# The second half of the last gate, computed as Strassen block products

## The chip, the cores and the metric

One core of a Trainium2 chip runs one launch of one layer of a decoder trunk. The metric is the device time of that launch in microseconds; several runs are summed up by their median. Engines are named as in the profile: PE multiplies matrices, DVE and ACT do elementwise work, POOL does a little arithmetic and issues some DMAs, SP issues most DMAs.

## The reference

Only the end of the layer matters here. `x` is the residual stream after the feed-forward block, 576 tokens (512 of the prompt, 64 of the samples) of 1024 channels.

```
x = x + _rmsnorm(f, g_ffn_post)                                    # f: the feed-forward block
x = x + jax.nn.sigmoid(_rmsnorm(x, g_ple) @ w_ple_gate) * (p_l @ w_ple_proj)
return x                                                           # y_prompt and y_sample
```

`w_ple_gate` is 1024x1024. It is "the last gate" of the title. All arithmetic is float32.

## The kernel before

**Layout.** Activations lie channel-major: a tile is 128 channels x 576 tokens, and each product runs over the two token halves of `H = 288` columns (half 0 and half 1). A product in float32 is made of three matmuls in the type fp32r, which split each operand into a high and a low part: high x high, high x low, low x high. A plain tile of 128 output channels by 576 tokens over 1024 input channels takes 8 x 3 x 2 = 48 matmuls of 288 columns. Weights come by SP's DMAs as raw float32 (`wst`), ACT makes the high part (`whi`, a cast), DVE the low part (`wlo`, a subtraction). Four `whi` and four `wlo` buffers of 1024 columns exist, so weights are made a few tiles ahead.

**Block products.** Most other matrix products of the kernel already use a Strassen scheme. `panels()` lists the weight tiles in their order; `two(a, b, kind)` marks two neighbouring output tiles as a pair. A pair cuts its problem into 2x2 blocks (two output tiles, two halves of the input channels, two token halves) and makes it with 7 block products of 12 matmuls instead of 8. It needs four weight blocks and four sums of weight blocks (class `Pair`), and, for each of four channel tiles, four sums of activations (class `Operands`). For a pair of kind "sum" the weight sums are made ahead in device memory by POOL's accumulating DMAs (`weight_sums`), eight for each pair of 256 KB, two at each `tick`; a tick is a tiny POOL copy that follows the cast of a weight tile. `Operands.make` takes channel tiles j and j + 4, makes four chained sums of 288 columns on DVE (`stmp`), and splits them into high (ACT) and low (DVE) parts (`xs`): the first sum alone, then the other three as one 864-column piece. `pairs()` runs the products; the results of the four blocks are called c11, c12 (in place in their PSUM banks), c21 and c22 (one more DVE subtraction, `value`).

**The last stage.** `handover(..., nxt)` ends the feed-forward block and starts the gate. It finishes four tiles of `f`, adds them into the residual (`residual`, lines 1149 and 1150), scales and splits the result by `g_ple` (`split_gain`, lines 578 and 579) into `XH`, `XL`, then runs the gate's tiles 0 to 3, first all four on half 0 (`pa`), then all four on half 1 (`pb`). Meanwhile `squares` sums the squares of the residual in `ssn` (DVE line 1132), and `stats(ssn, rn, i)` turns them into the factor 1/rms of half i: one matmul with a constant matrix into a PSUM bank (line 566), a DVE transpose out of that bank (548), a DVE step (554), a power on POOL (555), three DVE steps (556, 557, 560) and a transpose into `rn` (562). Only with `rn` can `evac_y` (lines 1260 to 1264) take a finished tile out of its PSUM bank: multiply by `rn` (DVE), tanh (ACT), two DVE steps with `pp` and the residual, a DMA to the output. The normalization is applied after the product, so the matmuls need no `rn`. There are 8 PSUM banks: 6 in the pool `psum`, 2 in `psb`. Tile 4 follows in `handover`, tiles 5 to 7 in the loop at the end; tile 7 is run half by half.

**What sets the order.** A scheduler places the instructions of each engine from dependencies, its own estimates and priorities (`tc.high_priority`). On the chip each engine then takes its list strictly in that order.

Of the kernel before, what the change touches and what calls it, by code (L numbers as in the profile page):

```python
# [9 lines left out]
AF = mybir.ActivationFunctionType  # L10
# [4 lines left out]
SKEW = 4  # L15
WARM = 10
T = 576
H = 288
# [11 lines left out]
def panels():  # L30

    out, items = [], []

    def cols(name, ms, k0=0):
        for m in ms:
            items.append((len(out), "one"))
            out.append([(name, k0 + k, m) for k in range(8)])

    def two(a, b, kind="pair", k0=0):
        items.append((len(out), kind))
        for name, m in (b, a):
            out.append([(name, k0 + k, m) for k in range(8)])

    def small(tiles):
        items.append((len(out), "one"))
        out.append(tiles)

    cols("rq", range(2))  # L50
    cols("rk", range(2))
    cols("rv", range(4))
    for t in (0, 2):
        two(("rg", t), ("rg", t + 1))
    for t in (0, 2):
        for n in ("cc", "ch", "cb"):
            two((n, t), (n, t + 1))
    for n in ("conv", "ret", "att"):
        if n == "ret":
            two(("ak", 0), ("av", 0))  # L60
            for t in (0, 2):
                two(("aq", t), ("aq", t + 1))
        for m in range(0, 8, 2):
            two(("g" + n, m), ("g" + n, m + 1))
            small([("b" + n, k, q) for q in (m, m + 1) for k in range(4)])
    cols("wo", range(8))
    small([("pp", k, m) for m in range(4) for k in range(2)])
    for c in range(4):
        if c == 0:
            cols("f1", range(8))  # L70
            cols("f2", range(8))
            continue
        for m in range(8 * c, 8 * c + 4):
            two(("f1", m), ("f1", m + 4), "sum")
        n = 4 if c < 3 else 2
        for m in range(n):
            two(("f2", m), ("f2", m + n), "pair" if m else "sum", 8 * c)
        cols("f2", range(2 * n, 8), 8 * c)
    small([("pp", k, m) for m in range(4, 8) for k in range(2)])
    cols("pg", range(8))  # L80
    return out, items


# [1 line left out]
def decoder_step(ctx: ExitStack, tc: tile.TileContext, xT, pT, W, consts, smalls, s0q, s0t, ckT, cv,  # L85
# [50 lines left out]
    def halft():  # L136
        return hlf.tile([P, H], F32, tag="hlf", name=nm("hlf"))
# [153 lines left out]
    def need(j, part=None):  # L291

        while not (j in wprep if part is None else j in made and part in made[j].w):
            next(make)
# [208 lines left out]
    def unit(w, xh, xl, kws, ks, half=None):  # L503
        ps = [mbank() if half in (None, i) else None for i in range(2)]
        n = len(ks)
        for q in range(n):
            mm(w, kws[q], ps, xh(ks[q]), xl(ks[q]), q == 0, q == n - 1)
            if q % 4 == 3:
                pump()
        return ps  # L510
# [100 lines left out]
    def later(fs):  # L611
        for f, a in fs:
            yield
            f(*a)
# [516 lines left out]
            A.activation(t, src, AF.Square)  # L1131
            V.tensor_tensor(out=ssx[:, HS[i]], in0=ssx[:, HS[i]], in1=t, op=ALU.add)

    def handover(hin, lin, evac, src, gn, tag, nxt):


        php = pp_inputs()
        pp = bigt(F32, "pp")
        pps.append(pp)
        XH, XL = Act8(F32R, "xh" + tag), Act8(F32R, "xl" + tag)  # L1140
        ra = cpool.tile([P, T], F32, tag="rb", name="ra" + tag)
        rn = npool.tile([P, T], F32, tag="rn", name="rn" + tag)
        ssn = npool.tile([P, T], F32, tag="ssn", name="ssn" + tag)

        def residual(i, ks):
            with tc.high_priority():
                for k in ks:
                    h, t = HS[i], halft()
                    V.tensor_tensor(out=t, in0=src(k)[:, h], in1=ra[:, h], op=ALU.mult)  # L1149
                    V.tensor_tensor(out=X1(k)[:, h], in0=X1(k)[:, h], in1=t, op=ALU.add)  # L1150
                    split_gain(X1(k)[:, h], gn, k, XH(k)[:, h], XL(k)[:, h])

        def squares(i):
            for k in range(8):
                addsq(ssn, X1(k)[:, HS[i]], i, k == 0)

        w = []
        for q in range(SKEW):
            w.append(nextw())
            evac(8 - SKEW + q, unit(w[q], hin, lin, ident_k, ident_k, 0), 0)  # L1160
        bg.append(later([(stats, (evac.ss, ra, 0))]))
        pump()
        for q in range(SKEW):
            ps = unit(w[q], hin, lin, ident_k, ident_k, 1)
            with tc.high_priority():
                evac(8 - SKEW + q, ps, 1)
            residual(0, ((), (0, 1), (2, 3), (4, 5))[q])
        wp = nextw()
        pp_unit(wp, 0, pp, *php)
        residual(0, (6, 7))  # L1170
        pp_unit(wp, 1, pp, *php)
        pp_unit(wp, 2, pp, *php)
        with tc.high_priority():
            stats(evac.ss, ra, 1)
        pp_unit(wp, 3, pp, *php)
        w, pa, pb = [], [], []
        for q in range(SKEW):
            w.append(nextw(2 if q < 2 else 0))
            residual(1, (2 * q, 2 * q + 1))
            pa.append(unit(w[q], XH, XL, ident_k, ident_k, 0))  # L1180
            if q == 2:
                squares(0)
        squares(1)
        for q in range(SKEW):
            pb.append(unit(w[q], XH, XL, ident_k, ident_k, 1))
            if q == 1:
                stats(ssn, rn, 0)
                for i in range(SKEW):
                    nxt(i, pa[i], rn, 0)
        need(items[pos[0]][0])  # L1190
        need(items[pos[0] + 1][0])
        bg.append(later([(stats, (ssn, rn, 1))]))
        pump()
        p4 = unit(nextw(), XH, XL, ident_k, ident_k)
        for q in range(SKEW):
            nxt(q, pb[q], rn, 1)
        for i in range(2):
            nxt(SKEW, p4, rn, i)
        return XH, XL, rn
# [55 lines left out]
                V.scalar_tensor_tensor(t[:, HS[i]], ps[i][:, :H], 0.0, r[:, HS[i]], op0=ALU.max, op1=ALU.mult)  # L1255
                squares_f(m, i, t[:, HS[i]])

    def evac_y(m, ps, r, i):
        z = halft()
        V.tensor_tensor(out=z, in0=ps[i][:, :H], in1=r[:, HS[i]], op=ALU.mult)  # L1260
        A.activation(z, z, AF.Tanh, scale=0.5)
        V.scalar_tensor_tensor(z, z, 1.0, pps[m // 4][:, m % 4, HS[i]], op0=ALU.add, op1=ALU.mult)
        V.tensor_tensor(out=X1(m)[:, HS[i]], in0=X1(m)[:, HS[i]], in1=z, op=ALU.add)
        nc.sync.dma_start(out=yT[:, m, HS[i]], in_=X1(m)[:, HS[i]])

    def block_tile(q, which):

# [94 lines left out]
        nc.sync.dma_start(out=X1.t[k], in_=dx[:, 4 * k:4 * k + 4, :])  # L1362
    nc.sync.dma_start(out=pps[0], in_=dpp)
    fhl = F[0].hi, F[0].lo
    XH, XL, rb = handover(*fhl, evac_f, f, 4, "3", evac_y)


    for m in range(SKEW + 1, 8):
        if m == 7:
            w = nextw()  # L1370
            ps = [unit(w, XH, XL, ident_k, ident_k, i)[i] for i in range(2)]
        else:
            ps = unit(nextw(), XH, XL, ident_k, ident_k)
        for i in range(2):
            evac_y(m, ps, rb, i)

# [111 lines left out]
```

## Time and the profile before

| | us |
|---|---|
| median of 3 runs | 986.15 (986.05 to 987.69) |
| profiled execution, its own time | 987.22 |
| span of the profiled execution, first to last instruction | 985.4 |
| PE busy | 957.6 (97%) |
| DVE busy | 712.6 (72%) |
| ACT busy | 531.5 (54%) |

The profiled execution is 1.07 us above the median. Its span leaves out 1.8 us of its own time. PE is busy nearly throughout; where DVE holds the chain, it is at stage borders.

### The profile page before, as it was taken

What the parts mean: (1) busy time and instruction counts of PE and PEld (TensorE: products, weight loads), DVE (VectorE), ACT (ScalarE), POOL (GpSimd) and SP (SyncE); (2) the same over time, 40 slices, a digit from 0 to 9 for tenths busy, and PEclk for the clock granted to TensorE, in tenths of its full rate; (3) what the DMA queues carried; (4) which work ended last, traced back from release to release, by engine and by line L of the source; (5) the groups of instructions that cost most, each with busy time, mean ns of one, the idle gap of its engine ahead of it and who ended that gap; (6) DMA issues with size and microseconds to landing.
All of it is one profiled execution on the core that took longest, in us unless ns stands there. A gap on an engine that the chain in (4) does not pass through costs nothing.

```text
span 985.4 us, 18290 instructions
## 1 busy us (share of the span) xinstructions
PE 957.6 (97%) x7081; PEld 925.0 (94%) x7081; DVE 712.6 (72%) x1308; ACT 531.5 (54%) x1051; POOL 187.1 (19%) x257
## 2 busy tenths in 40 slices
PE   9999999989989999999999999999999999999998
PEld 9999898989979888799999999999999999999897
DVE  7898789765576776577427878558847965785986
ACT  7345444433345564545436455468558845885642
POOL 0414443433324222332001100000010011000010
PEclk9999999999999999999999999999999999999999
DMA  8637565658779665688522532444486368593112
GB/s 301 168 86 199 165 138 146 163 164 220 194 218 248 143 153 153 143 226 252 187 66 71 223 108 100 155 148 145 120 199 192 110 153 222 164 356 109 65 62 79
DMA packets 65576, 160.45 MB, mean 163 GB/s; under 512 B 8089, under 2 KB 11193, under 8 KB 64241
## 3 DMA queue, kind: packets, MB, share of 16 engines
q1 hardware_dynamic: 48672, 114.75, 34.9%
q0 software_dynamic: 16672, 44.48, 21.8%
q8 instruction: 55, 0.90, 0.4%
q14 instruction: 33, 0.26, 0.1%
q10 hardware_dynamic: 144, 0.06, 0.0%
HBM read 139.17 MB, written 51.55 MB: 194 GB/s over the span
## 4 chain that ended last, share of the span: by engine, by line
PE 77%; DVE 13%; DMA 4%; ACT 2%; issue 2%; POOL 1%; SPq 0%; ACTq 0%; DVEq 0%; POOLq 0%
PE pm L501 31%; PE pbb L329 18%; PE pa L329 12%; PE pe L329 12%; DMA wst<-in_W 3%; DVE wlo L257 3%; POOL rs_b L555 1%; DVE hlf L1149 1%; DVE xl L579 1%; DVE x L1150 1%; DVE wst L227 1%; DVE s L952 1%; PE pb L964 1%; ACT whi L256 1%; DVE wlo L164 1%
## 5 line engine op out<-in xcount | busy, mean ns | idle before, releaser
L257 DVE TENSOR_TENSOR wlo<-wst,whi 128x1024 fp32r<-128x1024 f32 (+1 forms) x180 | 195.4, 1087 | 95.9 <-ACT whi L256 95.1
L256 ACT CAST whi<-wst 128x1024 fp32r<-128x1024 f32 (+1 forms) x180 | 168.3, 940 | 129.9 <-PE pe L329 29.9
L329 PE MATMUL pbb<-xs,whi 128*128 128x288 f32 x1080 | 227.1, 302 | 10.0 <-DVE akv L426 4.1
L329 PEld LDWEIGHTS pbb<-xs,whi 128*128 128x128 f32 x1080 | 174.9, 190 | 19.0 <-DVE akv L426 4.9
L329 PE MATMUL pbb<-xs,wlo 128*128 128x288 f32 x540 | 160.6, 297 | 0.0
L329 PE MATMUL pa<-fq,whi 128*128 128x288 f32 x720 | 147.7, 297 | 0.6 <-DVE fq L583 0.5
L329 PEld LDWEIGHTS pa<-fq,whi 128*128 128x128 f32 x720 | 116.0, 189 | 2.3 <-DVE fq L583 0.7
L329 PE MATMUL pa<-fq,wlo 128*128 128x288 f32 x360 | 106.8, 297 | 0.4 <-DVE wlo L257 0.4
L329 PEld LDWEIGHTS pbb<-xs,wlo 128*128 128x128 f32 x540 | 102.7, 190 | 0.0
L163 ACT CAST whi<-wst 128x1024 fp32r<-128x1024 f32 (+1 forms) x64 | 61.5, 965 | 70.9 <-PE pm L501 48.8
L501 PE MATMUL pm<-xl,whi 128*128 128x288 f32 x384 | 95.0, 299 | 1.5 <-DVE xl L579 1.4
L501 PE MATMUL pm<-xh,whi 128*128 128x288 f32 x384 | 94.9, 300 | 1.5 <-ACT xh L578 1.4
L501 PE MATMUL pm<-xh,wlo 128*128 128x288 f32 x384 | 93.5, 296 | 0.3 <-DVE wlo L164 0.3
L164 DVE TENSOR_TENSOR wlo<-wst,whi 128x1024 fp32r<-128x1024 f32 (+1 forms) x64 | 71.2, 1118 | 23.7 <-ACT whi L163 21.3
L268 POOL COPY pace<-whi 128x1 f32<-128x1 f32 x61 | 36.6, 600 | 240.8 <-ACT whi L256 190.3
L227 DVE TENSOR_TENSOR wst<-wst 128x512 f32<-128x512 f32 x90 | 61.1, 686 | 28.7 <-DMA wst<-in_W 28.0
L555 POOL TENSOR_TENSOR rs_b<-rs_a,mhalf 128x9 f32<-128x9 f32 (+2 forms) x15 | 34.8, 2322 | 222.7 <-DVE rs_a L554 222.7
L329 PE MATMUL pe<-xs,whi 128*128 128x288 f32 x360 | 73.5, 294 | 0.1
L329 PE MATMUL pe<-fq,whi 128*128 128x288 f32 x360 | 73.3, 296 | 0.0
L501 PE MATMUL pm<-fq,whi 128*128 128x288 f32 x384 | 70.4, 296 | 0.0
L329 PEld LDWEIGHTS pa<-fq,wlo 128*128 128x128 f32 x360 | 67.9, 189 | 1.9 <-DVE wlo L257 1.1
L501 PEld LDWEIGHTS pm<-xh,whi 128*128 128x128 f32 x384 | 65.7, 188 | 3.9 <-ACT xh L578 2.4
(280 smaller groups left out, 2025.6 us busy)
## 6 DMA issues: line engine op xcount, KB each, us to landing
wst<-in_W SPq DMA_DIRECT2D x86, 512.0 KB, 4.5
wst<-in_W SPq DMA_DIRECT2D x105, 256.0 KB, 3.3
ts<-in_W POOLq DMA_DIRECT2D x90, 256.0 KB, 5.7
wst<-ts SPq DMA_DIRECT2D x60, 256.0 KB, 3.3
ts<-ts POOLq DMA_DIRECT2D x30, 256.0 KB, 3.5
df<-tmp POOLq DMA_DIRECT2D x16, 288.0 KB, 5.1
x<-in_xT SPq DMA_DIRECT2D x10, 288.0 KB, 4.2
dacc<-tmp SPq DMA_DIRECT2D x8, 288.0 KB, 4.3
```

The lines of the kernel that those rows point to most:

```text
L163: A.copy(out=hi[:, c, :], in_=st[:, c, :])
L164: V.tensor_tensor(out=lo[:, c, :], in0=st[:, c, :], in1=hi[:, c, :].bitcast(F32), op=ALU.subtract)
L227: V.tensor_tensor(out=out, in0=a, in1=b, op=ALU.add)
L256: A.copy(out=hi, in_=r[:, :n, :])
L257: V.tensor_tensor(out=lo, in0=r[:, :n, :], in1=hi.bitcast(F32), op=ALU.subtract)
L268: t = G.tensor_copy(out=pace, in_=hi[:, 0, :1].bitcast(F32))
L329: PE.matmul(bank[:, :H], lhsT=lhs[:, s + j, :], rhs=rhs, start=start and j == 0 and i == 0, stop=j == 3 and i == 2, skip_group_check=True)
L501: PE.matmul(p[:, :H], lhsT=lhs[:, kw, :], rhs=r, start=s, stop=e)
L555: G.tensor_tensor(out=b, in0=a, in1=mhalf[:, :nb], op=ALU.pow)
L579: V.scalar_tensor_tensor(lo, src, gain(gi, k), hi.bitcast(F32), op0=ALU.mult, op1=ALU.subtract)
L952: V.scalar_tensor_tensor(s[:, h, :], dist, -SLOPES[h], p[g][:, i * w:i * w + w], op0=ALU.mult, op1=ALU.add)
L964: PE.matmul(po[grow(g), :], lhsT=avt[:, 128 * chunk + 64 * g:128 * chunk + 64 * g + 64], rhs=sb[g], start=kh == 0, stop=kh == nk - 1)
```

## The change

Tiles 0 to 3 of the gate stay plain. Tiles 4 to 7 become two pairs, (4, 6) and (5, 7), of kind "sum". Their weight sums join the list that POOL's DMAs make, at its end. In `handover`, while the four `pb` tiles are issued, ACT makes the scaled residual of channel tiles q and q + 4 (a copy of 576 columns scaled by the gain) and `Operands.make` makes the sums from it: four sets, q = 0 to 3. The residual's existing `XH`, `XL` serve as the plain blocks. After `stats` of half 1 the two pairs run by `pairs`, and the results go through `evac_y`. `evac_y` now works in a `tmp` buffer (five of 576 columns) instead of `hlf` (three of 288), writes the result there and sends it from there, so that the residual `X1` isn't overwritten while the sums still read it.

```diff
@@ panels()
     small([("pp", k, m) for m in range(4, 8) for k in range(2)])
-    cols("pg", range(8))
+    cols("pg", range(4))
+    for m in (4, 5):
+        two(("pg", m), ("pg", m + 2), "sum")
@@ handover
-    def handover(hin, lin, evac, src, gn, tag, nxt):
+    def handover(hin, lin, evac, src, gn, tag, nxt, sums=None):
...
         for q in range(SKEW):
             pb.append(unit(w[q], XH, XL, ident_k, ident_k, 1))
+            if sums:
+                t = [tmpt() for _ in range(2)]
+                for i in range(2):
+                    A.activation(t[i], X1(q + 4 * i), AF.Copy, scale=gain(gn, q + 4 * i))
+                sums.make(*[[z[:, h] for h in HS] for z in t])
             if q == 1:
                 stats(ssn, rn, 0)
                 for i in range(SKEW):
                     nxt(i, pa[i], rn, 0)
+        bg.append(later([(stats, (ssn, rn, 1))]))
+        pump()
+        if sums:
+            need(items[pos[0]][0], "b21")
+            pump()
+            sums.at = lambda i, k: (XH(k)[:, HS[i]], XL(k)[:, HS[i]])
+
+            def done(q, which):
+                if q.n == 0 and which == "c11":
+                    for i in range(SKEW):
+                        nxt(i, pb[i], rn, 1)
+                m, i = where(which)
+                z = None if which in ("c11", "c12") else halft()
+                evac_y(4 + q.n + 2 * m, None, rn, i, value(q, which, z))
+
+            pairs(2, sums, done, True)
+            rest()
+            return
         need(items[pos[0]][0])
         need(items[pos[0] + 1][0])
-        bg.append(later([(stats, (ssn, rn, 1))]))
-        pump()
         p4 = unit(nextw(), XH, XL, ident_k, ident_k)
@@ evac_y
-    def evac_y(m, ps, r, i):
-        z = halft()
-        V.tensor_tensor(out=z, in0=ps[i][:, :H], in1=r[:, HS[i]], op=ALU.mult)
+    def evac_y(m, ps, r, i, src=None):
+        z = tmpt()[:, :H]
+        V.tensor_tensor(out=z, in0=ps[i][:, :H] if src is None else src, in1=r[:, HS[i]], op=ALU.mult)
         A.activation(z, z, AF.Tanh, scale=0.5)
         V.scalar_tensor_tensor(z, z, 1.0, pps[m // 4][:, m % 4, HS[i]], op0=ALU.add, op1=ALU.mult)
-        V.tensor_tensor(out=X1(m)[:, HS[i]], in0=X1(m)[:, HS[i]], in1=z, op=ALU.add)
-        nc.sync.dma_start(out=yT[:, m, HS[i]], in_=X1(m)[:, HS[i]])
+        V.tensor_tensor(out=z, in0=X1(m)[:, HS[i]], in1=z, op=ALU.add)
+        nc.sync.dma_start(out=yT[:, m, HS[i]], in_=z)
@@ end of the kernel
-    XH, XL, rb = handover(*fhl, evac_f, f, 4, "3", evac_y)
-
-
-    for m in range(SKEW + 1, 8):
...
+    handover(*fhl, evac_f, f, 4, "3", evac_y, Operands(None))
```

How the order of instructions moves, at three places (lines of the changed kernel are shifted by 2 up to `handover` and by 23 in `evac_y`). First PE at the statistics of half 1, before: `pm_11326` and `pm_11327` are the two halves of tile 4, `pb_11352` the bank of the statistics.

```order
L501 MATMUL pm_11326<-xh_10568,wlo_11310 128x288
L501 MATMUL pm_11327<-xh_10568,wlo_11310 128x288
L566 MATMUL pb_11352<-ssn_10574,ones_d 128x288
L501 MATMUL pm_11326<-xh_10569,whi_11309 128x288
L501 MATMUL pm_11327<-xh_10569,whi_11309 128x288
```

PE at the same place, after: `pm_11318` is the last of the four `pb` tiles, `pa_11423` the first block product of the first pair.

```order
L503 MATMUL pm_11318<-xh_10601,whi_11008 128x288
L503 MATMUL pm_11318<-xl_10603,whi_11008 128x288
L503 MATMUL pm_11318<-xh_10601,wlo_11009 128x288
L568 MATMUL pb_11410<-ssn_10606,ones_d 128x288
L331 MATMUL pa_11423<-xh_10600,whi_11399 128x288
```

Half of tile 4 stood ahead of the statistics and is gone from there; the statistics follow the plain tiles directly. PE has 168 matmuls behind them in both kernels; ahead of them, back to the statistics of half 0, 70 before and 50 after, and 4 fewer ahead of those.

Second, DVE from the transpose of half 0's statistics to the factor `rn` of half 0, before (`wlo` is the low part of a weight tile).

```order
L548 STREAM_TRANSPOSE tmp_11223<-pb_11221 128x288
L1132 TENSOR_TENSOR ssn_10574<-ssn_10574,hlf_11168 128x288
L554 TENSOR_SCALAR rs_a_11225<-tmp_11223 128x9
L164 TENSOR_TENSOR wlo_11316<-wst_11314,whi_11315 128x1024
L556 SCALAR_TENSOR_TENSOR rs_d_11227<-rs_b_11226 128x9
L557 TENSOR_TENSOR rs_d_11227<-rs_d_11227,rs_a_11225 128x9
L560 SCALAR_TENSOR_TENSOR tmp_11223<-rs_d_11227,rs_b_11226 128x288
L562 STREAM_TRANSPOSE rn_10573<-tmp_11223 128x288
```

The same stretch of DVE after (`xs_11272` is the second set of activation sums, the `wlo` of line 259 are weights of the two pairs).

```order
L550 STREAM_TRANSPOSE tmp_11283<-pb_11281 128x288
L259 TENSOR_TENSOR wlo_11400<-wst_11396,whi_11399 128x1024
L585 TENSOR_TENSOR xs_11272<-stmp_11271,xs_11272 128x864
L556 TENSOR_SCALAR rs_a_11285<-tmp_11283 128x9
L259 TENSOR_TENSOR wlo_11407<-wst_11403,whi_11406 128x1024
L558 SCALAR_TENSOR_TENSOR rs_d_11287<-rs_b_11286 128x9
L259 TENSOR_TENSOR wlo_11499<-wst_11495,whi_11498 128x1024
L559 TENSOR_TENSOR rs_d_11287<-rs_d_11287,rs_a_11285 128x9
L259 TENSOR_TENSOR wlo_11518<-wst_11515,whi_11517 128x512
L562 SCALAR_TENSOR_TENSOR tmp_11283<-rs_d_11287,rs_b_11286 128x288
L259 TENSOR_TENSOR wlo_11525<-wst_11521,whi_11524 128x1024
L564 STREAM_TRANSPOSE rn_10605<-tmp_11283 128x288
```

Five weight splits and one split of activation sums now stand between the steps of that chain, where one weight split stood.

Third, DVE after, further on: the third and fourth sets (`xs_11348`, `xs_11387`) around the statistics of half 1. Before, nothing but `evac_y` and weight splits stood there.

```order
L585 TENSOR_TENSOR xs_11348<-stmp_11347,xs_11348 128x864
L562 SCALAR_TENSOR_TENSOR tmp_11412<-rs_d_11416,rs_b_11415 128x288
L368 TENSOR_TENSOR stmp_11386<-tmp_11382 128x288
L368 TENSOR_TENSOR stmp_11386<-tmp_11383,tmp_11382 128x288
L564 STREAM_TRANSPOSE rn_10605<-tmp_11412 128x288
L585 TENSOR_TENSOR xs_11387<-stmp_11386,xs_11387 128x288
L368 TENSOR_TENSOR stmp_11386<-tmp_11382,stmp_11386 128x288
L1283 TENSOR_TENSOR tmp_11450<-pm_11203,rn_10605 128x288
L368 TENSOR_TENSOR stmp_11386<-tmp_11383,stmp_11386 128x288
```

The last two sets of sums come on DVE behind the first `evac_y` steps, and so behind `rn` of half 0.

## Rows read from the trace of the kernel before

**Rows 1.** The page: busy us, share, instructions; the chain that ended last.
```profile
PE 957.6 (97%) x7081; PEld 925.0 (94%) x7081; DVE 712.6 (72%) x1308; ACT 531.5 (54%) x1051; POOL 187.1 (19%) x257
PE 77%; DVE 13%; DMA 4%; ACT 2%; issue 2%; POOL 1%; SPq 0%; ACTq 0%; DVEq 0%; POOLq 0%
```
**Rows 2.** The chain in order of time, last stage: start us, us, what.
```profile
930.35 0.74 DVE x L1150 x2
...
931.82 0.43 DVE xl L579
...
935.44 9.07 PE pm L501 x65
...
947.93 9.75 PE pm L501 x70
957.69 0.48 PE pb L566 x2
958.17 22.35 PE pm L501 x168
...
980.55 0.47 DVE hlf L1260
...
981.04 0.45 ACT hlf L1261
...
982.01 0.46 DVE x L1263
```
**Rows 3.** Stretches: us, then busy us of each engine, PE clock, DMA share, GB/s.
```profile
941.00:954.00 13.00, 12.99 (x92) 12.21 (x91) 10.74 (x26) 5.46 (x12) 2.64 (x1) 1.00 0.07 27
954.00:968.00 14.00, 14.00 (x104) 13.72 (x103) 11.86 (x30) 4.96 (x10) 1.80 (x1) 1.00 0.15 54
```
**Rows 4.** DVE in order of time: start us, us, what, [idle before <-releaser].
```profile
938.44 2.69 DVE L1132 TENSOR_TENSOR ssn<-ssn,hlf 128x288 f32<-128x288 f32 x5
...
946.84 1.23 DVE L164 TENSOR_TENSOR wlo<-wst,whi 128x1024 fp32r<-128x1024 f32 x1
947.99 0.45 DVE L1132 TENSOR_TENSOR ssn<-ssn,hlf 128x288 f32<-128x288 f32 x1
948.35 0.48 DVE L548 STREAM_TRANSPOSE tmp<-pb 128x288 f32<-128x288 f32 x1
...
949.09 0.17 DVE L554 TENSOR_SCALAR rs_a<-tmp 128x9 f32<-128x9 f32 x1
...
952.07 0.17 DVE L556 SCALAR_TENSOR_TENSOR rs_d<-rs_b 128x9 f32<-128x9 f32 x1 [1.69 <-POOL rs_b L555]
...
953.49 1.19 DVE L1260 TENSOR_TENSOR hlf<-pm,rn 128x288 f32<-128x288 f32 x3
...
960.69 0.16 DVE L554 TENSOR_SCALAR rs_a<-tmp 128x9 f32<-128x9 f32 x1
962.82 0.17 DVE L556 SCALAR_TENSOR_TENSOR rs_d<-rs_b 128x9 f32<-128x9 f32 x1 [1.97 <-POOL rs_b L555]
```
**Rows 5.** Groups by form, whole span: count, busy us, mean ns of one.
```profile
L583 DVE TENSOR_TENSOR xs<-stmp,xs 128x864 fp32r<-128x864 f32 x17 | 17.9, 1053 | 3.2 <-ACT xs L582 3.2
```
**Rows 6.** The power on POOL in the last stage, by tile: ns min/median/max.
```profile
L555 POOL TENSOR_TENSOR rs_b<-rs_a,mhalf x4: 1797/1878/2638, 907.3 to 961.0; 128x9 f32<-128x9 f32 x4
```
**Rows 7.** DMA issues: count, KB each, median us to landing.
```profile
wst<-ts SPq DMA_DIRECT2D x60, 256.0 KB, 3.3
ts<-in_W POOLq DMA_DIRECT2D x90, 256.0 KB, 5.7
out_yT<-x SPq DMA_DIRECT2D x16, 144.0 KB, 1.7
```
**Rows 8.** Stretches elsewhere, columns as in the third group.
```profile
118.00:124.00 6.00, 5.61 (x33) 5.61 (x34) 6.00 (x13) 2.09 (x4) 2.44 (x5) 0.73 0.34 103
460.00:480.00 20.00, 20.00 (x153) 20.00 (x152) 11.94 (x18) 9.61 (x15) 0.00 (x0) 1.00 0.84 293
```
**Rows 9.** PE where it stood longest before the clock fell: idle us before, releaser.
```profile
118.39 0.69 PE L721 MATMUL pb<-cst,rqk 128*128 128x128 f32 x2 [2.42 <-DVE bgt L690]
```

More of the change, by code (lines that the diff above doesn't have):

```diff
@@ L1364, in decoder_step @@
     fhl = F[0].hi, F[0].lo
-    XH, XL, rb = handover(*fhl, evac_f, f, 4, "3", evac_y)
-    for m in range(SKEW + 1, 8):
[L1369 to L1375, printed above, removed]
+    handover(*fhl, evac_f, f, 4, "3", evac_y, Operands(None))
 def _constants():
```

## The prediction

> **What bounds the kernel now.** The page comes first: PE is busy 97% of the span and holds 77% of the chain that ended last [rows 1]. A change that takes matmuls away therefore pays where PE holds the chain, and only as long as nobody else takes it over. So I read the chain through the last stage in order of time [rows 2]. Up to 935.4 it goes through DVE, which makes the residual. From 935.44 to 980.52 it is PE alone: 9.07 us for 65 matmuls, later 9.75 us for 70, the statistics of half 1 at 957.69, then 168 matmuls in 22.35 us, 0.133 us each. PE waits for nothing in these 45 us. The tail behind the last matmul runs from 980.55 to 982.47.
>
> How much room the helpers have is read from the stretches [rows 3]: DVE is busy 10.74 of 13.0 us and 11.86 of 14.0, so it has 2.3 + 2.1 = 4.4 us to spare between 941 and 968. ACT is not the problem (5 of 13 and 14). The reader should see that PE runs free here only because a nearly full DVE is just ahead of it.
>
> **What is removed.** Two pairs of 84 matmuls replace four tiles of 48: 24 matmuls, 24 x 0.133 = 3.2 us of PE. The order says where: 168 stand behind the statistics of half 1 in both kernels, and the 24 are missing ahead of them (70 become 50, and 4 more). So PE could reach these statistics at 957.69 - 3.2 = 954.5.
>
> **What is added on DVE.** Prices are start to start: 0.37 us for 288 columns (two take 0.74 in the chain), 0.43 for a scaled split [rows 2], 1.15 for a weight split of 1024 (946.84 to 947.99) [rows 4], so by the line between them 0.61 for 512; an 864-column split of sums lasts 1.053 [rows 5] and hands over 0.08 earlier, as the weight split does: 0.97. Four sets of four sums are 16 x 0.37 = 5.9, their splits 4 x (0.37 + 0.97) = 5.4, weights (six pieces of 1024 and two of 512 for four of 1024) 3.5, four `value` subtractions 1.5: 16.3 us on an engine with 4.4 us of room. That alone says DVE takes the chain; what it costs depends on who waits for which row.
>
> **First wait: a PSUM bank, behind `rn` of half 0.** Four `pa` and four `pb` tiles fill all 8 banks. The statistics of half 1 need one, so PE can't start them until `evac_y` has multiplied the first `pa` tile by `rn` of half 0. PE is in strict order: everything queued behind, the pairs included, waits too. Before, that multiplication started at 953.49 [rows 4], with PE still 4 us from the statistics. After, by the order, DVE does from the first add of squares at 938.44 to the transpose: 14 adds, 8 sums, 2 short splits and 4 residual steps (28 x 0.37 = 10.4), 2 scaled splits (0.9) and a long split (1.0): 12.2 us. The same stretch before (13 adds, 4 + 2 residual steps, one weight split: 8.3 us of work) took 9.9, so 1.6 went to gaps between adds that depend on one another (five take 2.69, not 1.9 [rows 4]). The sums stand between the adds and fill such gaps; I take 0.5, bounds 0 and 1.6. The transpose comes at 951.1 instead of 948.35.
>
> From the transpose to the first `evac_y` the trace has 5.14 us [rows 4], with one weight split hidden under POOL's power. After, a weight split and a long split stand ahead of the step that feeds the power, where one add stood (1.15 + 0.97 - 0.37 = 1.75), and three weight pieces between the steps behind it (1.15 + 0.61 + 1.15 = 2.9). That is 9.8 us with the power of that row, the longest of four at 2.64, and 9.0 with the shortest, 1.80 [rows 6]. I take 9.4. The first `evac_y` multiplication starts at 960.5 and ends at 960.95; the statistics of half 1 start at 961.0, 3.3 us later than before, after PE has waited 6.5. The saving is used up here and as much again is lost.
>
> The Trainium skill, Perfetto Trace Analysis, section Optimizing Tensor Performance (Matmuls), says that independent matmul groups should rotate through PSUM banks so that the evacuation of one overlaps the next one's matmuls; by that rule this change is wrongly placed, because eight banks hang on one late factor. Before, the trace shows the rule kept (no PE wait in the chain). Where evacuations kept pace, the sum would be the first rival's below.
>
> **Second wait: the last two sets of sums.** From 960.5 to the end of the fourth set DVE does 8 + 4 + 4 steps of `evac_y`, 8 sums and 2 short splits (26 x 0.37 = 9.6), 2 long splits (1.9), one 512-column weight piece (0.6), two transposes and one step (1.2), and stands still for the second power: 2.13 to 2.98 from the step that feeds it to the next [rows 4], I take 2.5 with the small step behind it. That is 15.8. The chained sums with ACT's casts between them, and the `tmp` buffers that now wait until an output DMA has landed (1.7 us [rows 7]), cost nothing at best; dependent steps cost 0.19 more each, as in the adds above, and five or so stand in this stretch: 1.0, bounds 0 and 1.9. The last split ends at about 977.3. By then PE has been able to do only the 70 matmuls of its order that don't need it (9.3 us of work since 961.5), so it idles some 6.5 us here. 98 remain: 98 x 0.133 = 13.1, plus waits for ACT's copies of `pe` and `pbb`, which the order puts behind four tanh of at most 0.45 us each [rows 2]: 0 to 1.8, I take the middle, 0.9. The last matmul ends at 991.3 instead of 980.52: +10.7.
>
> **Tail.** Before, four steps of 0.46 follow the last matmul, 1.92 us. After, DVE has five short steps of two other blocks and its own ahead of the last one (5 x 0.37 + 0.48 = 2.3): +0.4. The DMA behind it is of the same size.
>
> **Elsewhere.** 16 more DMAs of POOL (5.7 us to landing each [rows 7]) run at 460 to 500, where the first 20 us use 0.84 of the DMA time and PE is busy throughout [rows 8]. Plain weight tiles are made two ahead there, 2 x 6.4 us of PE work. I cost them at nothing; 1 us if a weight comes late. POOL's next urgent work, the power, lies at 520 and later. SP issues 14 loads of 256 KB (3.3 us [rows 7]) for 4 of 512 KB while DMA is at 0.07 to 0.15 [rows 3]: nothing, but the weight pieces in front of `rn` wait for them, up to 0.5.
>
> **The sum.** PE's work -3.2, first wait +6.5, second wait +6.5, copies +0.9, tail +0.4: +11.1. Against the profiled execution: 987.22 + 11.1 = 998.3. That execution was 1.07 above the median of its kernel, so against the median: 986.15 + 11.1 = **997.3 us**. With all gaps, copies and POOL's power at their lower bounds it is +7.9 (994.1), at their upper bounds and with the late load +15.4 (1001.6).
>
> **Rivals.** (1) The sums are covered: `rn` of half 0 is ready in time and PE never waits. Then -3.2 + 0.4, 983.4, faster. It decides at 954.5: the first `evac_y` would have to end 6.5 us earlier than my sum. For it speaks that PE has 3 us less to do and ACT much room; against it that DVE would need 16.3 us where it has 4.4. (2) Only the bank is waited for, since the scheduler filled later gaps: +3.3 + 0.4 = 989.9, still slower by 0.4%; it needs the fourth set at 970.8, 6.5 us earlier on the same DVE. With the bank wait halved as well it would be 986.6, no change. (3) The clock falls. In 118 to 124 PE stood idle 2.42 us behind DVE [rows 9], and the granted clock of that stretch was 0.73, that is partly 1.2 instead of 2.4 GHz: 6.0 x 0.27 = 1.6 us lost [rows 8]. My forecast leaves PE idle for 6.5 us. A slow clock right behind that wait is hidden, since PE then waits for DVE anyway; if it lasts into the 98 remaining matmuls it costs 1.6 to 3.2: 998.9 to 1000.5. The Trainium skill, TensorE: Matmul & The Clock Gate, Part 1, has this as a rule: an idle array falls back to half its clock and activity releases it; the row agrees. (4) The 16 DMAs delay weights at 460 to 500: +1 on top. That the change doesn't do what it says is excluded by the order: 6848 matmuls instead of 6872.
>
> **How the numbers follow.** Forecast 0.70, clock rival 0.15, late weights 0.03, bank alone 0.07 (of which no change 0.03), sums covered 0.05. About 0.2%, 2 us, can be told from no change. Faster 0.05, same 0.03, slower 0.92. The range holds the forecast's bounds and the clock rival, and a little below for sums that DVE fits in better: 992 to 1003. It leaves out rivals 1 and 2 and some tails.
>
> **What would show it.** In the profile after: a PE wait of about 6 us at the statistics of half 1, released by DVE `evac_y`, the largest; further PE waits of 0.3 to 2 us on `xs` and on ACT's copies, 7 us in all; `rn` of half 0 done near 960; DVE over 85% busy from 938 to 977; the last matmul near 991. I am wrong if PE shows no wait at those statistics, or if the waits lie with DMA.

## The result, and the profile after

The changed kernel takes 1000.37 us in the median of 4 runs (996.14 to 1004.21), the kernel before beside it 986.10 (986.05 to 987.69): ratio 1.0139, 95% interval 1.0117 to 1.0162. It is slower by 14 us. The profiled execution is the slowest of the four, 1004.21 us, with a span of 1002.1.

First its page: busy time, share and instructions of each engine, then the chain that ended last. Against [rows 1] PE holds 71% of the chain instead of 77%, DVE 16% instead of 13%.

```profile
PE 963.6 (96%) x7057; PEld 929.1 (93%) x7057; DVE 727.9 (73%) x1340; ACT 546.8 (55%) x1077; POOL 209.8 (21%) x281
...
PE 71%; DVE 16%; DMA 5%; ACT 2%; issue 2%; POOL 2%; SPq 0%; POOLq 0%; DVEq 0%; ACTq 0%
```

PE's waits from 930 us on: who waited for whom, us in total, times, the longest. Before there was none in this stage behind 935.44 [rows 2].

```profile
PE pb L568 <- DVE tmp L1283: 6.0, 1, 6.0
PE pbb L331 <- DVE xs L585: 1.8, 2, 1.3
...
PE pe L331 <- ACT xs L584: 0.4, 1, 0.4
...
PE pbb L331 <- ACT pbb L453: 0.3, 1, 0.3
```

DVE in order of time (start, us, what). The first add of squares, which stood at 938.44 [rows 4], is at 944.70: the stage begins 6.26 us later than before. The rows behind it are to be read with that taken off.

```profile
944.70 0.46 DVE L1134 TENSOR_TENSOR ssn<-ssn,hlf 128x288 f32<-128x288 f32 x1
...
956.86 0.47 DVE L550 STREAM_TRANSPOSE tmp<-pb 128x288 f32<-128x288 f32 x1
...
966.31 1.19 DVE L1283 TENSOR_TENSOR tmp<-pm,rn 128x288 f32<-128x288 f32 x3
...
981.81 1.06 DVE L585 TENSOR_TENSOR xs<-stmp,xs 128x864 fp32r<-128x864 f32 x1 [0.23 <-ACT xs L584]
```

PE in order of time around its long wait, and at the end. The matmuls from 968.19 on stand 0.24 us apart instead of 0.133.

```profile
966.83 1.33 PE L568 MATMUL pb<-ssn,ones_d 128*128 128x288 f32 x2 [5.99 <-DVE tmp L1283]
...
968.19 0.45 PE L331 MATMUL pa<-xl,whi 128*128 128x288 f32 x1
968.43 0.45 PE L331 MATMUL pa<-xh,wlo 128*128 128x288 f32 x1
...
996.48 0.29 PE L331 MATMUL pbb<-xs,wlo 128*128 128x288 f32 x1
```

Stretches (us, then busy us of each engine, PE clock, DMA share, GB/s); the first two answer to [rows 3] and what lies behind them, the last one lies far ahead of the stage. PE lost its clock behind the 6-us wait, and also between 480 and 500.

```profile
954.00:968.00 14.00, 7.32 (x48) 6.56 (x47) 12.27 (x25) 6.71 (x12) 2.64 (x1) 0.88 0.40 132
968.00:980.00 12.00, 9.99 (x58) 9.08 (x56) 9.86 (x26) 6.01 (x11) 1.80 (x1) 0.86 0.14 49
480.00:500.00 20.00, 17.71 (x120) 17.25 (x119) 8.16 (x11) 7.67 (x14) 5.10 (x8) 0.91 0.75 223
```

Behind the 6 us in which PE stood, the granted clock was 0.50 (1.2 of 2.4 GHz) from 967.0 to 971.4; from there on it was whole again up to 997.

So the profiled loss has two places. **The last stage:** from the first add of squares to the end of DVE's last step before took 982.47 - 938.44 = 44.03 us [rows 2, 4]; after 999.10 - 944.70 = 54.40: +10.4. **Ahead of it** 6.3 us were lost, 4.3 of them between 465 and 495 us.

### The profile page after: what moved, and what is told of

It reads as the page before. It is cut to its first block, busy times and chain, and to the rows that moved or that the text cites. A ratio compares the mean times of both kernels' runs of the same rounds, so it can differ in the third digit from the quotient of the medians.

```text
span 1002.1 us, 18372 instructions
## 1 busy us (share of the span) xinstructions
PE 963.6 (96%) x7057; PEld 929.1 (93%) x7057; DVE 727.9 (73%) x1340; ACT 546.8 (55%) x1077; POOL 209.8 (21%) x281
## 4 chain that ended last, share of the span: by engine, by line
PE 71%; DVE 16%; DMA 5%; ACT 2%; issue 2%; POOL 2%; SPq 0%; POOLq 0%; DVEq 0%; ACTq 0%
PE pm L503 25%; PE pbb L331 19%; PE pa L331 12%; PE pe L331 11%; DMA wst<-in_W 4%; DVE wlo L259 3%; POOL rs_b L557 2%; DMA tmp<-dacc 1%; DVE wlo L166 1%; DVE wst L229 1%; DVE xl L581 1%; DVE hlf L1151 1%; DVE x L1152 1%; DVE stmp L368 1%; DVE xs L585 1%
## 5 line engine op out<-in xcount | busy, mean ns | idle before, releaser
L331 PE MATMUL pbb<-xs,whi 128*128 128x288 f32 x1128 | 238.8, 303 | 10.3 <-DVE tmp L428 3.8
L331 PEld LDWEIGHTS pbb<-xs,whi 128*128 128x128 f32 x1128 | 183.8, 191 | 20.7 <-DVE tmp L428 5.2
L331 PE MATMUL pbb<-xs,wlo 128*128 128x288 f32 x564 | 168.4, 299 | 0.0
L331 PEld LDWEIGHTS pbb<-xs,wlo 128*128 128x128 f32 x564 | 107.9, 191 | 0.0
L270 POOL COPY pace<-whi 128x1 f32<-128x1 f32 x69 | 48.8, 708 | 265.3 <-ACT whi L258 192.9
L503 PE MATMUL pm<-xh,whi 128*128 128x288 f32 x320 | 79.3, 300 | 2.3 <-ACT xh L580 1.5
L503 PE MATMUL pm<-xl,whi 128*128 128x288 f32 x320 | 79.8, 299 | 1.5 <-DVE xl L581 1.4
L331 PE MATMUL pe<-xs,whi 128*128 128x288 f32 x376 | 77.7, 296 | 0.9 <-ACT xs L584 0.4
L503 PE MATMUL pm<-xh,wlo 128*128 128x288 f32 x320 | 78.1, 296 | 0.3 <-DVE wlo L166 0.3
L1347 POOL DMA_DIRECT2D df<-tmp x16 | 13.8, 861 | 244.3 <-DVE tmp L1343 160.5
```

The source lines that it names most:

```text
L270: t = G.tensor_copy(out=pace, in_=hi[:, 0, :1].bitcast(F32))
L331: PE.matmul(bank[:, :H], lhsT=lhs[:, s + j, :], rhs=rhs, start=start and j == 0 and i == 0, stop=j == 3 and i == 2, skip_group_check=True)
L503: PE.matmul(p[:, :H], lhsT=lhs[:, kw, :], rhs=r, start=s, stop=e)
L1347: G.dma_start(out=df[m], in_=q.t[m2], accum_op=ALU.add)
```

## The experiments

All kernels' runs scatter by some 4 us to either side (the kernel before: 982.3 to 992.0 in 23 runs), by what the traces show mostly through low-clock stretches in the first 300 us, where all kernels do the same. A median of six runs can't settle 2 us then; the trace can, since the same two instructions can be found in each: the five kernels of the table that give DVE the changed kernel's work in the changed kernel's order agree to 0.1 us in the stage. The table gives the stage as above, from the first add of squares to the end of DVE's last step, and the medians with that of the kernel before in the same series.

| kernel | first add | end | stage, against 44.03 | median (before) | ratio, 95% |
|---|---|---|---|---|---|
| changed | 944.70 | 999.10 | +10.4 | 1000.37 (986.10) | 1.0117-1.0162 |
| after_again | 938.58 | 992.96 | +10.4 | 999.73 (987.07) | 1.0114-1.0174 |
| dma_only | 939.85 | 983.87 | 0.0 | 988.11 (986.48) | 0.9991-1.0037 |
| late_sums | 940.32 | 994.78 | +10.4 | 999.93 (986.48) | 1.0105-1.0169 |
| mid_sums | 940.20 | 994.66 | +10.4 | 997.56 (987.64) | 1.0085-1.0130 |
| free_late | 938.18 | 992.63 | +10.4 | 999.45 (986.48) | 1.0113-1.0168 |
| one_set_late | 940.09 | 985.63 | +1.5 | 989.85 (986.48) | 1.0017-1.0059 |
| sums_idle | 938.09 | 989.37 | +7.3 | 992.92 (987.07) | 1.0047-1.0088 |
| no_sums | 936.24 | 979.83 | -0.4 | 986.15 (987.07) | 0.9980-1.0020 |
| b4_free | 940.56 | 993.19 | +8.6 | 996.48 (987.64) | 1.0063-1.0113 |
| b4 | 937.90 | 991.24 | +9.3 | 996.21 (987.07) | 1.0079-1.0124 |
| wpool | 938.64 | 1002.87 | +20.2 | 1008.29 (987.64) | 1.0191-1.0241 |
| spool | 939.02 | 996.00 | +13.0 | 1003.42 (987.64) | 1.0136-1.0195 |

### Is it the 16 DMAs? dma_only, late_sums, mid_sums, after_again

**dma_only**, the kernel before with the DMAs alone:

```diff
-        todo = [j for j, kind in items if kind == "sum"]
+        todo = [j for j, kind in items if kind == "sum"] + [len(plan) - 4, len(plan) - 2]
```

> The kernel before, and beside it only the 16 weight-sum DMAs of POOL for four matrices of the last gate, at the place where the change puts them (about 460 to 500 us); nobody reads what they make. Theory 'collision': in the changed kernel's profile DVE's lag against the kernel before grows from about 1.8 to 6.3 us between 446 and 483 us, where DMA was already at 0.84 of its time, so the DMAs alone cost 3 to 5 us: 989 to 991, with runs some us apart, PE idle for 1 to 3 us between 470 and 495, the accumulated gate's loads landing later. Rival 'nothing' (the prediction's term, 0 to 1 us): 986.1 to 987.1, and the lag seen was that one execution's.

**late_sums** and **mid_sums**, the changed kernel with the DMAs held back (99 and 66 are places in the tile list):

```diff
         for a in range(0, len(gens), 3):
+            while a == 15 and items[pos[0]][0] < 99:     # mid_sums: 66
+                yield True
```

> The changed kernel with the same 16 DMAs issued after the tile list has passed the fourth pair of the second feed-forward block (about 610 us and later, where DMA is at 0.42 to 0.47 of its time). Theory 'collision': about 4 us come back: 995 to 998, and the runs lie closer together than the 8 us of the changed kernel; the last stage looks as in the changed kernel, with its wait of 6 us at the statistics of half 1. Rival 'nothing': 1000.4 with the same scatter.

> The changed kernel with the 16 extra DMAs held back only until the output projection begins (from about 475 to 525 us), where DMA is at 0.24 and 0.18 of its time from 480 on. Theory 'collision': DVE's lag against the kernel before, read in the traces between the same instructions, grows by less than 0.6 us from 460 to 700 us (changed kernel: 4.3; the DMAs alone: 1.1; late_sums 1.4 at 690 to 735, where DMA is at 0.72 to 0.84). Rival 'every DMA of POOL costs, wherever it lies': again 1.0 to 1.4. In both cases the last stage is +10.4 as in the changed kernel; time 996 to 998 against 986.5.

**after_again** is the changed kernel.

> The changed kernel unaltered, once more, with more runs. Theory 'collision': the last stage is again +10.4 (three altered kernels had 10.43 in their traces), and DVE's lag grows by 1 to 4.5 us between 460 and 500: 11.5 to 15 above the kernel before, 1 to 4 us above what mid_sums had (+9.9). Rival 'one execution': the lag grows by under 0.5 us there, and the time is within 1 us of +10.

DVE's lag against the profiled kernel before, at the same instruction, grows from 465 to 495 us by 4.3 in the changed kernel, 1.1 in dma_only, 0.0 in late_sums and mid_sums, and 0.0 in after_again. late_sums loses 1.4 us up to 735, most of it near 690, where its DMAs then lie (free_late 1.3, one_set_late 0.9, the same DMAs). With the DMAs where mid_sums has them, neither it nor no_sums, b4, wpool and spool loses more than 0.2 us at either place (b4_free 0.4). Several expectations were missed here: dma_only lies between its two theories (1.1 us of lag instead of 3 to 5, 988.11 us), late_sums got nothing back in the median (999.93 instead of 995 to 998), and after_again has the lag of its rival but not the rival's time.

What waits at 465 to 495 us is the accumulated gate, a sum over three branches of the layer that is kept in device memory (`dacc`): `tmp<-dacc` are four loads of SP that fetch it back, and the add of line 1097 (1095 in the kernels made from the one before, 1099 in mid_sums) waits for them. From 440 to 500 us, the add's group (count | busy us, mean ns | idle before, released by) in the kernel before:

```profile
L1095 DVE TENSOR_TENSOR tmp<-tmp,tmp 128x576 f32<-128x576 f32 x6 | 4.5, 754 | 0.1
```

In dma_only:

```profile
L1095 DVE TENSOR_TENSOR tmp<-tmp,tmp 128x576 f32<-128x576 f32 x6 | 4.5, 755 | 2.9 <-DMA tmp<-dacc 2.8
```

In the changed kernel:

```profile
L1097 DVE TENSOR_TENSOR tmp<-tmp,tmp 128x576 f32<-128x576 f32 x6 | 4.5, 755 | 4.6 <-DMA tmp<-dacc 4.5
```

In mid_sums:

```profile
L1099 DVE TENSOR_TENSOR tmp<-tmp,tmp 128x576 f32<-128x576 f32 x6 | 4.5, 754 | 0.1
```

The loads themselves (DMA issues of the same stretch: count, KB, median us to landing), in the kernel before, then in the changed kernel:

```profile
tmp<-dacc SPq DMA_DIRECT2D x4, 288.0 KB, 6.4
```

```profile
tmp<-dacc SPq DMA_DIRECT2D x4, 288.0 KB, 10.4
```

PE's longest wait in that stretch of the changed kernel:

```profile
PE pm L503 <- ACT mh L1098: 2.0, 1, 2.0
```

In dma_only the loads took 9.3 us, in after_again 8.8, in mid_sums 6.1. They land 2.4 to 4.0 us later beside the DMAs and DVE stands waiting; with the DMAs moved away both are as before. That much is shown. How much of it reaches PE differs: in after_again DVE stood 1.0 us and PE didn't wait at all; in the changed kernel's first profile PE waited 2.3 us and the clock then stood at 0.91 for 20 us (1.8 us). So the collision costs 0 to 4.3 us in the executions that were seen.

The medians of the table give its mean price roughly. What is left when the stage is taken off the difference of the medians is 1.6, 2.3 and 3.9 us with the DMAs at the place of the change (dma_only, after_again, changed), 1.9 to 3.1 with them late (late_sums, free_late, one_set_late), and -0.5 to +0.5 with them where mid_sums has them (mid_sums, b4_free, b4, no_sums, wpool). sums_idle, which has none of them, leaves -1.5, so one such number alone is unsure by that much; the three groups together speak for 2 to 3 us at either of the first two places and nothing at the third.

### Bank or DVE? free_late

```diff
             pa.append(unit(w[q], XH, XL, ident_k, ident_k, 0))
+            if sums:
+                A.copy(out=pc[:, q, :H], in_=pa[q][0][:, :H])
+                pa[q] = [pc[:, q, :]]
```

> As late_sums, but ACT copies each of the four half-0 tiles of the last gate out of PSUM as soon as it is finished, so that their banks come free without waiting for the factor of half 0. Theory 'DVE work': PE's wait of 6 us at the statistics of half 1 vanishes and comes back as large at the operand sums of the third and fourth set, because DVE reaches these in the same place of its queue; the time stays within 1 us of late_sums. Rival 'banks' (the prediction's first wait taken as a cost of its own, +6.5 of PE idle): the wait is saved, 3.3 to 6.5 us less than late_sums.

The wait at the bank is gone and a wait of 5.5 us stands at the sums. PE's waits from 930 us on:

```profile
PE pe L333 <- ACT xs L586: 5.5, 1, 5.5
PE pbb L333 <- DVE xs L587: 1.2, 1, 1.2
```

The stage is +10.4 as before, to 0.1 us. In this kernel the bank is where PE happens to stand, not what it pays for: DVE's last split of the fourth set starts 37.1 us behind the first add with or without it.

### What of DVE's work? one_set_late, sums_idle, no_sums

**one_set_late** (`if sums and q: sums.s.append(sums.s[0])` in place of three of the four `sums.make`).

> As late_sums, but only the first of the four sets of operand sums is made and used four times, which leaves 12 sums and their 6 splits out of the computation (tiles 4 to 7 of the last gate come out as other numbers). DVE has 12 x 0.37 + 3 x (0.37 + 0.97) = 8.5 us less to do; PE does the same. Theory 'DVE work': the end comes 7 to 10 us earlier than late_sums, 986 to 990, the wait at the statistics of half 1 falls from 6 to 2 to 3 us. Rival 'weight pieces' (the eight weight splits of the two pairs hold DVE and PE, not the sums): 0 to 4 us earlier. Rival 'clock' (the clock that falls behind the 6-us wait is what costs): 2 to 3 us earlier.

The stage falls from +10.4 to +1.5, 8.9 us for 8.5 us of DVE's work, and the bank wait from 6.0 to 2.5. With the sums go ACT's copies and casts for them, so the run doesn't part DVE from ACT; ACT had room before [rows 3]. The weight splits are all still there, so that rival doesn't hold. The clock can't be the main cost either, but what is left is its price: in 954 to 968 us the granted clock was 0.88, 14 x 0.12 = 1.7 us, lost behind the wait of 2.5 with PE busy all the time, and -3.2 + 2.5 + 1.7 is 1.0 of the 1.5.

**sums_idle** (the `sums` block of `handover` put into the kernel before, `Operands(None)` handed over, nothing else).

> The kernel before, and in its last stage only the four sets of operand sums and their splits, at the place where the change has them; nobody reads them, tiles 4 to 7 stay plain. DVE gets 5.9 + 5.4 = 11.3 us of work where it had 4.4 us of room between 941 and 968. Theory 'DVE's work': PE waits at the statistics of half 1 for a bank although it needs none of the sums, and the end comes 5 to 9 us later. Rival 'operands' (PE loses time only where it reads sums that aren't ready): 0 to 1 us later.

+7.3 us, for sums that nobody reads. DVE's and PE's row in order of time: `rn` of half 0 is first used at 959.16 instead of 953.49 [rows 4] (the first add stands at 938.09 instead of 938.44), and PE stands 5.5 us for it.

```profile
959.16 1.19 DVE L1265 TENSOR_TENSOR hlf<-pm,rn 128x288 f32<-128x288 f32 x3
```

```profile
959.76 0.88 PE L501 MATMUL pm<-xh,whi 128*128 128x288 f32 x2 [5.53 <-DVE hlf L1265]
```

The rest is mostly clock. In 954 to 968 us 14 x 0.12 = 1.7 us of clock were lost, nearly all of them behind that wait, where PE has work and nothing else to wait for:

```profile
954.00:968.00 14.00, 8.47 (x52) 8.15 (x52) 10.55 (x26) 6.62 (x11) 2.94 (x2) 0.88 0.12 42
```

So here the wait at the bank is paid in full, since no later wait covers it. Whether freed banks would save it in this kernel was not tried.

**no_sums** (`sums.s` filled with views of `XH` and `XL`).

> As mid_sums, but no operand sum is made: the products take plain halves of the residual stream in their place (tiles 4 to 7 of the last gate come out as other numbers). The two pairs, their weights from the DMA sums, the four differences and the 24 matmuls less stay. one_set_late stood at +1.5 in the last stage; another set less is 2.8 us of DVE's work: theory 'DVE's work' gives -1.3, at best the -2.8 of the rival 'sums covered' in the prediction (-3.2 + 0.4), at worst +0.5 where the weight splits keep PE waiting. Rival 'pairs' (the chained banks of the pairs and ACT's copies cost by themselves): +2 or more.

-0.4 us. With the sums free DVE is busy 11.3 of 13 and 12.2 of 14 us, and PE's waits in the stage behind 941 us are 0.2 to 0.5 us each. These are the stretches:

```profile
941.00:954.00 13.00, 12.76 (x90) 12.01 (x89) 11.32 (x27) 8.08 (x16) 2.64 (x1) 1.00 0.33 103
954.00:968.00 14.00, 12.79 (x91) 11.86 (x90) 12.24 (x29) 6.47 (x14) 2.64 (x1) 1.00 0.33 109
```

Of the 3.2 us of matmuls that the pairs save, 0.4 then arrive at the end; the median shows no difference from the kernel before. The pairs, their weights, the four differences and `evac_y` in its new buffers are all in this kernel, so none of these explains the loss of the changed one. Even with free operands there was next to nothing to gain, and the sums alone cost more than twice the saving.

### Can the order or another engine help? b4_free, b4, wpool, spool

**b4_free** and **b4** make all four sets in the first two rounds of the `pb` loop, ahead of `stats(ssn, rn, 0)`; b4_free also has the copies of free_late.

```diff
-            if sums:
+            if sums and q < 2:
+                for j in (2 * q, 2 * q + 1):     # scale and sums.make of set j
```

> As mid_sums, with the half-0 tiles copied out of PSUM by ACT (as in free_late), and all four sets of operand sums written ahead of the statistics and the evacuations of half 0, so that DVE does them first and the evacuations later. DVE's work is the same. Theory 'order' (the end is set by when the fourth set is split, as the prediction's second wait has it: 98 matmuls or 13.1 us behind it): the fourth set is ready 8 to 12 us earlier, and the end comes 6 to 9 us earlier. Theory 'sum of DVE's work' (whatever is done first, what is put off is waited for instead: weight splits, then the factor of half 1): PE's waits only change their places, the end comes 0 to 2 us earlier than +10.4.

> As b4_free, all four sets ahead of the statistics of half 0, but without the copies out of PSUM. The factor of half 0 now comes later and the bank with it. Theory 'DVE's work': PE stands at the bank for 6 to 9 us instead of at the sums and weights behind it, and finds all sums ready then; the last stage is +7.5 to +9.5, as in b4_free (+8.6). Rival 'banks': without free banks the late factor is paid on top: +10.4 or more.

1.8 and 1.1 us come back of 10.4. In b4 the fourth set's last split stands at 964.54 (26.6 us behind the first add; 37.1 in the changed kernel), yet the end is only 1.1 us earlier: now the factor of half 0 comes later and PE waits 6.9 us for it and another 1.7 behind it; the sums are ready by then, as forecast for this run.

```profile
PE pb L570 <- DVE tmp L1286: 6.9, 1, 6.9
PE pa L333 <- DVE tmp L1286: 1.7, 1, 1.7
```

The slow clock behind these waits costs b4 another 2.5 us or so (granted 0.63 in 954 to 968, with PE busy for 5.40 of the 14 us). In b4_free the fourth set is split 27.1 us behind the first add, 10 us earlier than in the changed kernel; PE's waits are spread over its cast by ACT (`xs`) and ACT's copies of blocks (`pbb`, `pe`):

```profile
PE pbb L333 <- ACT xs L586: 2.5, 1, 2.5
PE pbb L333 <- ACT pbb L455: 1.9, 1, 1.9
PE pbb L333 <- ACT pe L468: 1.2, 1, 1.2
```

What DVE does first decides where PE waits, hardly how long: all gaps of PE in the stage add up to 9.7 us in the changed kernel, 9.6 in b4 and 7.5 in b4_free.

**wpool** (line 259: `E = G if j >= 144 else V; E.tensor_tensor(...)`, the low parts of the two pairs' weights on POOL) and **spool** (line 368: the sums on POOL).

> As mid_sums, but the lower parts of the two pairs' weights (six pieces of 1024 columns, two of 512; 8.1 us of DVE's work) are split by POOL instead of DVE. What POOL takes for such a piece no row shows yet. Theory 'sum of DVE's work': the last stage comes 3 to 6 us earlier than +10.4, the bank wait falls from 6 to 2 to 4 us, provided that POOL's piece takes under 2.5 us. Rival 'sums': 8.1 us of work that PE doesn't wait for directly bring 0 to 1 us. Rival 'POOL': its pieces stand ahead of its power for the factor, which then comes 1 to 3 us later: no gain or a loss.

> As mid_sums, but the 16 operand sums (not their splits) are made by POOL instead of DVE: 5.9 us of DVE's work go. Theory 'sum of DVE's work': if POOL takes at most twice DVE's 0.37 us for a sum, the end comes 3 to 6 us earlier. Rival 'chain': from 1 us for a sum on, the fourth set comes later than now, since the sums of a set depend on one another and go to and fro between POOL, ACT and DVE: 0 to 4 us later than mid_sums; and DVE's own short steps beside POOL's get longer if the two hinder each other.

Both are much worse than DVE doing it: +20.2 and +13.0 (spool lost 2 us more ahead of its first add). No theory named a loss as large as wpool's. In wpool POOL took 3.1 us for a piece that takes DVE 1.15, where the gain hung on less than 2.5. The trace of wpool in order of time, POOL and DVE:

```profile
949.46 7.90 POOL L262 TENSOR_TENSOR wlo<-wst,whi 128x1024 fp32r<-128x1024 f32 x2 [4.07 <-ACT whi L260]
...
952.32 1.85 DVE L559 TENSOR_SCALAR rs_a<-tmp 128x9 f32<-128x9 f32 x1
...
957.32 1.80 POOL L560 TENSOR_TENSOR rs_b<-rs_a,mhalf 128x9 f32<-128x9 f32 x1
...
959.08 3.56 POOL L262 TENSOR_TENSOR wlo<-wst,whi 128x1024 fp32r<-128x1024 f32 x2
959.15 2.29 DVE L561 SCALAR_TENSOR_TENSOR rs_d<-rs_b 128x9 f32<-128x9 f32 x1 [4.01 <-POOL rs_b L560]
```

Two prices are to be seen. The power at 957.32 waits behind a weight piece, 3.2 us after `rs_a` is there (952.32 + 1.85). And DVE's tiny steps, 0.16 and 0.17 us in the kernel before [rows 4], take 1.85 and 2.29 while POOL works. In spool it is the same with smaller pieces: POOL's groups (busy, mean ns) and DVE in order of time.

```profile
L371 POOL TENSOR_TENSOR stmp<-tmp,stmp 128x288 f32<-128x288 f32 x8 | 7.3, 917 | 0.6
L371 POOL TENSOR_TENSOR stmp<-tmp 128x288 f32<-128x288 f32 x4 | 3.9, 984 | 23.4 <-ACT tmp L1194 15.9 <-DVE xs L588 7.5
```

```profile
932.57 2.97 DVE L1155 TENSOR_TENSOR x<-x,hlf 128x288 f32<-128x288 f32 x3
933.37 1.85 POOL L371 TENSOR_TENSOR stmp<-tmp,stmp 128x288 f32<-128x288 f32 x2
```

Three residual adds take 2.97 us, where one by one they are 0.37 us apart [rows 2]. None of the twelve kernels beats the kernel before; the best forms of the change that leave nothing out, b4 and b4_free, stay 9 us behind it. Giving part of DVE's work to ACT, which is busy for 12.7 of the 26 us in 954 to 980 of the changed kernel, was not tried.

## Why the prediction was right, and where it wasn't

The prediction said 997.3 us (992 to 1003) and slower; it was 1000.37. Step by step, with the stage's 6.26 us of delay taken off:

- **DVE takes the chain: right, and shown.** sums_idle and one_set_late put 7.3 and 8.9 us on the sums (with their splits, casts and copies), and no_sums leaves nothing for the rest of the change. The transpose was forecast for 951.1 and stood at 950.6: the gaps that were put at 0.5 us are 0. From the transpose to the first `evac_y` 9.45 us were measured (956.86 to 966.31) for 9.4, with POOL's power at its longest, 2.64. So 960.05 for 960.5.
- **First wait: right in place and size, wrong in what it means.** PE waited 6.0 us at the statistics of half 1 for `evac_y`; forecast 6.5. But the text took the bank as the cause ("eight banks hang on one late factor") and 6.5 us as a term of the sum, and free_late shows that free banks change nothing. The sum survived since its end was worked out from DVE's last split, not from the two waits added up. By the same run the Trainium skill's advice that the prediction weighed (Perfetto Trace Analysis, Optimizing Tensor Performance, Matmuls: rotate banks so that evacuations overlap) was no remedy here: with four of the banks freed by ACT's copies PE waited 5.5 us elsewhere.
- **Second wait: right for this order of DVE's work.** From the first `evac_y` to the end of the fourth set 16.6 us (966.31 to 982.87) for 16.8 forecast. The 6.5 us of PE idle that were expected here came as 2.6 us of waits and 2.2 us of slow clock instead; the rest, under 2 us, isn't accounted for. That the fourth set as such sets the end is not so: made 10 us earlier (b4, b4_free) it brings 1.1 and 1.8 us.
- **The clock rival: the reading was right.** 14 x 0.12 + 12 x 0.14 = 3.4 us of clock were lost in 954 to 980. Some 1.2 of them fall into the wait itself; in the 4.4 us behind it (967.0 to 971.4) the clock was at 0.50, which is 2.2 us. They lie ahead of the fourth set, where PE waits for DVE anyway, and cost nothing at the end: in mid_sums PE's matmuls lost about 4.7 us to the clock, and the stage is the same +10.4. Where no such wait follows, in sums_idle and one_set_late, the clock is paid. The Trainium skill, TensorE: Matmul & The Clock Gate, Part 1, says that an idle array falls to half its clock; the rows agree (matmuls 0.24 apart right behind the wait, 0.133 later).
- **The last matmuls, the tail: right.** From the end of the fourth set to the last matmul's end 13.9 us (982.87 to 996.77) for 14.0. From there to the end 2.3 for 1.9 before: the +0.4.
- **The stage in all:** +10.4 for +11.1. The forecast of 997.3 is thus 3.1 us short: 0.7 too much in the stage, and 3.9 too little elsewhere (the numbers are rounded).
- **"Elsewhere": mis-sized.** The 16 DMAs were costed "at nothing; 1 us if a weight comes late", with a chance of 0.03. The row behind it was right (DMA at 0.84 in the first 20 us [rows 8]), but the text looked at the weights alone. Late were the loads of the accumulated gate, which share that stretch; in the profiled execution that cost 4.3 us, in others 1.1 and 0. Stage and collision make 986.1 + 10.4 + (0 to 4.3) = 996.5 to 1000.8, which holds the median. The medians speak for 2 to 3 us; that the collision is the whole of the 3.9 us between 996.5 and 1000.37 is not shown.
- **Rival "sums covered" (983.4): excluded** by sums_idle. Even no_sums reaches only -0.4.

## What to carry over

A block product pays for its saved matmuls with operand sums on an elementwise engine; compare the two in the stage where they run (here 3.2 us of PE against 16.3 us of DVE, which had 4.4 to spare), not over the whole kernel. A PE wait names the resource at which PE stands; before easing it, follow the releasing engine's queue to the end, since a full engine only moves the wait. And DMAs that are added "in the background" are to be held against every load that is due in that stretch, not only against the one they serve.

## What the runs showed of the hardware

- POOL is no relief for DVE here. 1024-column differences took it 3.1 us on average (DVE 1.15 from start to start), 288-column sums 0.92 to 0.98 (0.37). While it worked, DVE's 9-column steps took 1.85 and 2.29 us instead of 0.16 and 0.17. The Trainium skill, SBUF — State Buffer, section Who interferes with whom, has a rule for it: a DVE instruction with two SBUF inputs, or in a mode that uses two ports, and a GpSimd instruction that reads SBUF need the same port, and the one that comes second is held up for the whole instruction. The rows of wpool agree: the step of 2.29 us has two SBUF inputs, starts 0.07 us behind the first of two pieces of POOL and ends at 961.44, when that piece is done (961.42).
- SP's loads of 288 KB went from 6.4 to 8.8, 9.3 and 10.4 us when POOL's DMAs of 256 KB ran beside them at a DMA share that rose from 0.84 to between 1.02 and 1.05 in 460 to 480 us.
